# Modulation steps of three chunks on GpSimd's queue, and products that move from GpSimd to VectorE and ScalarE

## The chip, the core and the metric

The kernel runs on one core of a Trainium2 chip. TensorE (PE in the profile) multiplies matrices, VectorE (DVE) and ScalarE (ACT) work on rows of 128 partitions, GpSimd (POOL) does both arithmetic and the issuing of transfers, and SyncE (SP) only issues transfers. The metric is the device time of one execution in microseconds (us), lower is better; the time of a kernel is the median of its runs.

## The reference

Two residual networks run one after the other on 256 tokens of width 1024, all in float32. The first has two layers of differential attention beside a Hyena convolution. The second has an even layer (forgetting attention and gated linear attention, then a dense SwiGLU) and an odd layer (an s5 state-space mixer, then a mixture of eight experts). Every sublayer of the second network is modulated by a conditioning vector `c`:

```python
def adaln(c, w, b):
    m = jax.nn.silu(c.astype(jnp.float32)) @ w + b      # w: 1024 x 3072
    shift, scale, gate = jnp.split(m, 3, axis=-1)
    return shift[:, None, :], scale[:, None, :], gate[:, None, :]

def second_block(x, c, ...):
    # four modulations: e_mod_mix, e_mod_ffn, o_mod_mix, o_mod_ffn
    sh, sc, g = adaln(c, e_mod_mix_w[j], e_mod_mix_b[j])
    h = rmsnorm(x, e_norm_mix[j]) * (1.0 + sc) + sh
    y = even_mixer(h, ...)
    x = x + (g * y).astype(x.dtype)
    # then the same with the dense swiglu, the s5 mixer and the experts
```

The modulations depend on `c` alone, so they may be computed at any time before their use. The s5 mixer's parameters (powers of a complex decay, two matrices B and C per state, tables of cosines and sines) depend on weights alone, and may also be computed early.

## The kernel before

The text of the program is turned into one instruction list per engine by a scheduler that simulates the engines; an engine then works through its list in order. Weights arrive on SyncE's queue as [128 x 1024] chunks (`wchunk`). Each is split into a high part `whi` on ACT (L207) and a low part `wlo` on DVE (L210), and each product is three matmuls (L220 to L222, and L322 to L324 where the weight stands still).

By the trace, the first network runs until about 570 us, the even mixer from 640 to 765 us, the dense SwiGLU (the dense FFN below) from about 765 to 1010 us, the s5 mixer from 1060 to 1200 us, and the experts fill the rest.

**Background tasks.** Work that isn't due yet is written as a Python generator. `tick()` is called after each piece of a projection and lets each task take `rate` steps; `finish()` runs a task to its end. The four modulations are such a task (`modulations`, `adaln`) within the first network, at a rate of 0.65 steps for each tick, and `self.finish(self.adalns)` stands ahead of `w_out` of the first network's second layer. One modulation is 24 chunks of [128 x 1024]. A step takes two chunks (`ADA_STEP`). A chunk is fetched by SyncE's queue into `rawm` (L942, three buffers), and multiplied in eight pairs of instructions, 16 on PE in the profile's count (L947). After each four chunks ACT copies the result (L952), PE transposes it in four pieces (L955), and DVE adds up (L956). At the end of a modulation PE transposes the gate (L963), and a DMA writes it out as a row, from which GpSimd's queue later broadcasts `mgt` to all partitions (L200). A modulation has 13 steps; with the eight that are skipped at the start there are 60.

**The s5 parameters** are a task beside the even mixer and the dense FFN. For each of four quarters q it computes B (L1461 transposes, L1463 masks), C (four complex products by `cmul`, L1330 to L1338, on DVE, then masks L1477 and L1483 on POOL) and the tables T. A table is built by six complex products that double its length, all on POOL, and its one buffer is stored to memory as `sT` (L1522) by SyncE's queue before the next quarter's may be begun (POOL sets its first column at L1514, ACT fills its third part at L1520).

**The mixers.** In the gated linear attention POOL multiplies `gz` by `gq` and `gk` (L1104, L1105, L1132) and `gg` by `gn` (L1225). In the s5 mixer it does four additions per quarter beside two scans of DVE (L1559, L1562, L1575, L1576).

Of the kernel before, what the change touches and what calls it, by code (L numbers as in the profile page):

```python
# [118 lines left out]
class Net:  # L119
    def __init__(self, ctx, tc, a, out):  # L120
        self.ctx, self.tc, self.nc, self.a, self.out = ctx, tc, tc.nc, a, out
        self.uid, self.ring, self.extra, self.left, self.hold, self.held = 0, {}, 0, 0, None, 0
        self.tasks = []
        self.dq = (tc.nc.gpsimd, tc.nc.sync, tc.nc.scalar)[DQ]
# [801 lines left out]
    def adaln(self, key, pool, raw_alloc):  # L926
# [8 lines left out]
        bc = self.load(self.sm, a[key + "_c"], [P, 4, 8], "adb", bufs=1, eng=self.dq)  # L935
        ad = self.t(self.sm, [P, 24], "adv", bufs=1)
        silu = self.silu_cols(pool)
        for m0 in range(0, 24, 4):
            acc = self.psB()
            for m in range(m0, m0 + 4):  # L940
                raw = raw_alloc()
                nc.sync.dma_start(raw, w[m])  # L942
                cs = slice((m - m0) * P, (m - m0 + 1) * P)
                for r in range(2):
                    for j in range(4):
                        k = 2 * j + r
                        nc.tensor.matmul(acc[32 * j:32 * j + 32, cs], silu[:, k:k + 1].broadcast_to([P, 32]),  # L947
                                         raw[:, k * P:(k + 1) * P], start=r == 0 and m == m0, stop=r == 1, skip_group_check=True)
# [7 lines left out]
            V.tensor_reduce(ad[:, m0:m0 + 4], pt.rearrange("p (m j r) -> p m j r", m=4, j=4)[:, :, :, 0], AX.X, ALU.add)  # L956
            yield
        V.tensor_tensor(cols[:, 1], ad[:, 0:8], bc[:, 0], ALU.add)
# [7 lines left out]
        self.dq.dma_start(row.rearrange("(m n) -> m n", n=P), r)  # L966
# [13 lines left out]
    def modulations(self):  # L980
        raw = lambda: self.t(self.b1, [P, D], "rawm", bufs=AR_BUFS)
        for _ in range(ADA_SKIP):
            yield
        for k in ("e_mod_mix", "e_mod_ffn", "o_mod_mix", "o_mod_ffn"):
            yield from self.adaln(k, self.b1, raw)
            if k == "e_mod_ffn":
                for _ in range(ADA_SKIP1):
                    yield

    def adaln_task(self, key, pool, rate):  # L990
        return self.task(self.adaln(key, pool, self.raw), rate)
# [74 lines left out]
    def gla(self, b2, qT, kT, v, la, gg, yT):  # L1066
# [28 lines left out]
        for lv in range(6):  # L1095
# [8 lines left out]
            nc.gpsimd.tensor_tensor(zv[:, :, h:], zv[:, :, h:], qf.rearrange("p (n t) -> p n t", t=B)[:, :, h:], ALU.mult)  # L1104
            nc.gpsimd.tensor_tensor(zv[:, :, :h], zv[:, :, :h], kf.rearrange("p (n t) -> p n t", t=B)[:, :, :h], ALU.mult)  # L1105
# [6 lines left out]
        for lv in (6, 7):  # L1112
# [17 lines left out]
            for c in range(4):  # L1130
                second = c % 2 if lv == 6 else c // 2
                nc.gpsimd.tensor_tensor(zv[:, :, c, :], zv[:, :, c, :], (q4 if second else k4)[:, :, c, :], ALU.mult)  # L1132
# [30 lines left out]
    def even_mixer(self, b2):  # L1163
# [56 lines left out]
        def emit_gg(tt, c, p):  # L1220
# [4 lines left out]
            nc.gpsimd.tensor_tensor(v4, v4, gn[:, None, :].broadcast_to([P, 4, P]), ALU.mult)  # L1225
# [206 lines left out]
    def s5_params(self, sp):  # L1432
# [8 lines left out]
        for q in range(4):  # L1441
# [28 lines left out]
            for t in range(4):  # L1470
# [11 lines left out]
            for g in range(2):  # L1482
                nc.gpsimd.tensor_tensor(cm[:, 0, :, g, :], craw[:, 0], m2[:, None, g, :].broadcast_to([P, 8, 16]), ALU.mult)  # L1483
# [579 lines left out]
```

## Time and profile before

| | |
|---|---|
| Median of 3 runs | 1993.03 us (1983.26 to 1996.6) |
| The profiled execution | 1992.76 us, of which the span is 1991.0 us |
| Granted TensorE clock, mean of the span | 0.95 |
| PE, DVE, ACT, POOL busy | 94%, 78%, 60%, 10% |

The profiled execution is within the runs. Busy shares are means over stages with different limits, so the rows below are cut by stage. A matmul's listed length overlaps the next one's; how far PE moved is read from the starts. In a row of the timeline the bracket at the end is the time for which the engine was idle before, and what ended that.

### The profile page before, as it was taken

How to read it: one execution, taken by the hardware profiler on the slowest of the kernel's cores; microseconds unless marked ns; L12 is line 12 of the kernel's file. 1: busy time of each engine (PE TensorE's matmuls, PEld its weight loads, DVE VectorE, ACT ScalarE, POOL GpSimd, SP SyncE). 2: the span in 40 equal slices, each digit the busy share in tenths (PEclk: the TensorE clock that was granted, in tenths of full speed). 3: DMA queues.
4: the chain of work that ended last, by engine and by line, in shares of the span. 5: the costliest groups of instructions: out<-in, count | busy, mean ns of one | idle time of the engine just before them, and what ended most of it. 6: DMA issues, size and time to landing. Idle time of an engine off the chain costs nothing.

```text
span 1991.0 us, 31217 instructions
## 1 busy us (share of the span) xinstructions
PE 1869.4 (94%) x11450; PEld 1580.4 (79%) x11450; DVE 1555.7 (78%) x2484; ACT 1190.1 (60%) x1628; POOL 196.9 (10%) x319
## 2 busy tenths in 40 slices
PE   7899989999976998889988989999999999999997
PEld 6787767887754977779978978888888888888875
DVE  6687577686432756788878678999999999999897
ACT  6564445554322843434445358787788877877775
POOL 0000000000010011872212210010001000100000
PEclk9999999999977987999999789999999999999999
DMA  8635656755687631557666568999999999999991
GB/s 259 193 121 171 209 177 210 253 161 191 221 280 237 174 102 51 173 210 234 216 238 251 216 238 282 374 323 377 352 369 316 379 353 378 324 382 357 356 346 57
DMA packets 254826, 503.37 MB, mean 253 GB/s; under 512 B 20082, under 2 KB 97396, under 8 KB 252616
## 3 DMA queue, kind: packets, MB, share of 16 engines
q1 hardware_dynamic: 253848, 498.47, 72.5%
q0 software_dynamic: 816, 2.82, 0.4%
q8 instruction: 92, 1.51, 0.3%
q14 instruction: 70, 0.57, 0.1%
HBM read 485.47 MB, written 15.75 MB: 252 GB/s over the span
## 4 chain that ended last, share of the span: by engine, by line
PE 77%; DVE 8%; DMA 6%; issue 3%; POOL 3%; ACT 3%; SPq 0%; ACTq 0%; DVEq 0%; POOLq 0%
PE A L220 12%; PE A L222 12%; PE A L221 12%; PE B L220 6%; PE B L221 6%; PE B L222 6%; PE A L322 3%; PE A L323 3%; PE A L324 3%; PE B L947 3%; DVE wlo L210 2%; DMA k<-in_flt_deltas_dram 1%; DMA rawm<-in_o_mod_ffn_w_dram 1%; PE B L1743 1%; PE B L439 1%
## 5 line engine op out<-in xcount | busy, mean ns | idle before, releaser
L210 DVE TENSOR_TENSOR wlo<-raw,whi 128x1024 fp32r<-128x1024 f32 x777 | 935.0, 1227 | 190.1 <-ACT whi L207 178.7
L207 ACT ACTIVATE whi<-raw 128x1024 fp32r<-128x1024 f32 x777 | 813.5, 1057 | 369.9 <-PE A L222 141.6
L221 PE MATMUL A<-wlo,hTh 128*128 128x512 f32 (+1 forms) x752 | 288.6, 384 | 1.6 <-DVE wlo L210 1.3
L220 PE MATMUL A<-whi,hTh 128*128 128x512 f32 (+1 forms) x752 | 285.4, 387 | 4.2 <-ACT hTh L207 4.2
L222 PE MATMUL A<-whi,hTl 128*128 128x512 f32 (+1 forms) x752 | 286.9, 383 | 0.9 <-DVE hTl L210 0.9
L322 PE MATMUL A<-hTh,whi 128*128 128x256 f32 x864 | 248.4, 288 | 7.7 <-ACT whi L207 4.3
L324 PE MATMUL A<-hTh,wlo 128*128 128x256 f32 x864 | 246.6, 285 | 1.4 <-DVE wlo L210 1.4
L323 PE MATMUL A<-hTl,whi 128*128 128x256 f32 x864 | 246.8, 286 | 1.0 <-DVE hTl L210 1.0
L322 PEld LDWEIGHTS A<-hTh,whi 128*128 128x128 f32 x864 | 167.1, 193 | 12.0 <-ACT whi L207 4.5
L323 PEld LDWEIGHTS A<-hTl,whi 128*128 128x128 f32 x864 | 167.3, 194 | 3.6 <-issue 1.4
L324 PEld LDWEIGHTS A<-hTh,wlo 128*128 128x128 f32 x864 | 167.2, 193 | 3.7 <-DVE wlo L210 1.8
L220 PEld LDWEIGHTS A<-whi,hTh 128*128 128x128 f32 x752 | 141.7, 189 | 35.4 <-ACT hTh L207 4.9
L221 PEld LDWEIGHTS A<-wlo,hTh 128*128 128x128 f32 x752 | 141.8, 189 | 33.3 <-DVE wlo L210 4.9
L222 PEld LDWEIGHTS A<-whi,hTl 128*128 128x128 f32 x752 | 142.0, 189 | 31.0 <-DVE hTl L210 2.0
L221 PE MATMUL A<-wlo,xg 128*128 128x512 f32 (+1 forms) x384 | 143.5, 374 | 0.0
L222 PE MATMUL A<-whi,xg 128*128 128x512 f32 (+1 forms) x384 | 143.0, 372 | 0.0
L220 PE MATMUL A<-whi,xg 128*128 128x512 f32 (+1 forms) x384 | 141.7, 376 | 0.0
L221 PE MATMUL B<-wlo,mhh 128*128 128x512 f32 x352 | 138.7, 394 | 0.0
L222 PE MATMUL B<-whi,mhl 128*128 128x512 f32 x352 | 137.6, 391 | 0.0
L220 PE MATMUL B<-whi,mhh 128*128 128x512 f32 x352 | 120.9, 394 | 0.2 <-ACT mhh L207 0.2
L947 PE MATMUL B<-rawm,silu 128*32 128x128 f32 x1536 | 70.8, 312 | 22.0 <-DMA rawm<-in_o_mod_ffn_w_dram 14.3
L947 PEld LDWEIGHTS B<-rawm,silu 128*32 128x32 f32 x1536 | 45.0, 122 | 47.8 <-DMA rawm<-in_o_mod_ffn_w_dram 20.6
(575 smaller groups left out, 2974.1 us busy)
## 6 DMA issues: line engine op xcount, KB each, us to landing
raw<-in_o_exp_up_dram SPq DMA_DIRECT2D x176, 512.0 KB, 5.8
raw<-in_o_exp_down_dram SPq DMA_DIRECT2D x176, 512.0 KB, 6.1
raw<-in_o_exp_gate_dram SPq DMA_DIRECT2D x174, 512.0 KB, 5.7
raw<-in_w_in_dram SPq DMA_DIRECT2D x96, 512.0 KB, 5.1
rawm<-in_e_mod_mix_w_dram SPq DMA_DIRECT2D x24, 512.0 KB, 3.7
rawm<-in_e_mod_ffn_w_dram SPq DMA_DIRECT2D x24, 512.0 KB, 6.6
rawm<-in_o_mod_mix_w_dram SPq DMA_DIRECT2D x24, 512.0 KB, 4.9
raw<-in_e_w_in_dram SPq DMA_DIRECT2D x24, 512.0 KB, 4.2
```

Source lines behind the costliest of these rows:

```text
L207: nc.scalar.activation(hi, src, AF.Copy)
L210: (nc.gpsimd if lo_eng == "pool" else nc.vector).tensor_tensor(lo, src, hi.bitcast(F32), ALU.subtract)
L220: nc.tensor.matmul(out, ah, bh, start=first, stop=False)
L221: nc.tensor.matmul(out, ah, bl, start=False, stop=False)
L222: nc.tensor.matmul(out, al, bh, start=False, stop=last)
L322: nc.tensor.matmul(o, wh[:, ms], xh[:, k, :], start=k == 0 and m == 0, stop=False, **kw)
L323: nc.tensor.matmul(o, wh[:, ms], xl[:, k, :], start=False, stop=False, **kw)
L324: nc.tensor.matmul(o, wl[:, ms], xh[:, k, :], start=False, stop=k == 7, **kw)
L439: nc.tensor.matmul(o, x[:, ks], dg, start=True, stop=True)
L947: nc.tensor.matmul(acc[32 * j:32 * j + 32, cs], silu[:, k:k + 1].broadcast_to([P, 32]), raw[:, k * P:(k + 1) * P], start=r == 0 and m == m ...
L1743: nc.tensor.transpose(ptr[:, i * P:(i + 1) * P], sg[:, i * P:(i + 1) * P], self.ident)
```

## The change

1. **Modulations.** A step is now three chunks, and nothing is yielded inside it. The next step's three chunks are issued on GpSimd's queue (`self.mq`) right after this step's matmuls. The matmuls and ACT's copy of [128 x 384] are written under high priority. In place of four transposes per four chunks, four small DMAs of GpSimd's queue put one row of each of the four partial sums into `parts` [96 x 128], and one transpose and one reduction per modulation finish it. A modulation is 10 steps; with the eight skipped there are 48. The rate is 0.80. The three buffers of `rawm` stay.
2. **Gated linear attention.** The products with `gq`, `gk` and `gn` go to DVE.
3. **s5 parameters.** The masks of C (72 operations on [128 x 128]) go to ACT as copies with a scale per partition. The complex products of the tables T go to DVE, 144 operations.
4. **s5 mixer.** The four additions per quarter go to DVE.

Lines in the changed file are one to eleven higher (L947 is L959, the new DMAs are L965, the one transpose is L970). The core of the diff:

```diff
-    def adaln(self, key, pool, raw_alloc):
+    def adaln(self, key, pool, raw_alloc, bufs):
...
+        parts = self.t(self.sm, [96, P], "adp", bufs=1)
...
-        for m0 in range(0, 24, 4):
+        def fetch(m0):
+            raws = [raw_alloc() for _ in range(bufs)]
+            for i in range(bufs):
+                self.mq.dma_start(raws[i], w[m0 + i])
+            return raws
+
+        raws = fetch(0)
+        yield
+        for m0 in range(0, 24, bufs):
             acc = self.psB()
-            for m in range(m0, m0 + 4):
-                raw = raw_alloc()
-                nc.sync.dma_start(raw, w[m])
-                cs = slice((m - m0) * P, (m - m0 + 1) * P)
-                for r in range(2):
-                    for j in range(4):
...
-                if m % ADA_STEP == ADA_STEP - 1 and m < m0 + 3:
-                    yield
-            s = self.t(pool, [P, 512], "ads", bufs=1)
-            nc.scalar.activation(s, acc, AF.Copy)
-            pt = self.psB()
-            for i in range(4):
-                nc.tensor.transpose(pt[:, i * P:(i + 1) * P], s[:, i * P:(i + 1) * P], self.ident)
-            V.tensor_reduce(ad[:, m0:m0 + 4], ...)
+            with self.first():
+                for i in reversed(range(bufs)):
+                    cs = slice(i * P, (i + 1) * P)
+                    for r in range(2):
+                        for j in range(4):
...
+                s = self.t(pool, [P, bufs * P], "ads", bufs=1)
+                nc.scalar.activation(s, acc[:, :bufs * P], AF.Copy)
+            for j in range(4):
+                self.mq.dma_start(parts[24 * j + m0:24 * j + m0 + bufs], s[32 * j:32 * j + 1].rearrange("o (m p) -> o m p", m=bufs))
+            if m0 + bufs < 24:
+                raws = fetch(m0 + bufs)
             yield
+        pt = self.psB()
+        nc.tensor.transpose(pt[:, 0:96], parts, self.ident[0:96, 0:96])
+        V.tensor_reduce(ad, pt[:, 0:96].rearrange("p (j m) -> p m j", j=4), AX.X, ALU.add)
...
-            nc.gpsimd.tensor_tensor(zv[:, :, h:], zv[:, :, h:], qf..., ALU.mult)
+            nc.vector.tensor_tensor(zv[:, :, h:], zv[:, :, h:], qf..., ALU.mult)
...
-                        nc.gpsimd.tensor_tensor(C[:, :, ri, t, g, :], v, m2[:, None, g, :].broadcast_to([P, 8, 16]), ALU.mult)
+                        nc.scalar.activation(C[:, :, ri, t, g, :], v, AF.Copy, scale=m2[:, g, 0:1])
...
-                          T[:, 0, :, n:2 * n], T[:, 1, :, n:2 * n], f"s5rt", eng=nc.gpsimd)
+                          T[:, 0, :, n:2 * n], T[:, 1, :, n:2 * n], f"s5rt")
...
-            nc.gpsimd.tensor_tensor(t[0], t[0], t[1], ALU.add)
+            V.tensor_tensor(t[0], t[0], t[1], ALU.add)
...
-ADALN_RATE = 65
+ADALN_RATE = 80
```

**How the order moves.** First PE's list where the first network ends and the even mixer begins. `rawm` is a fetched chunk, `silu` the conditioning vector, `ads` the copied partial sums, `dg` and `x` the normalised input of the next projection, `adb` the gate. Before:

```order
L947 MATMUL B_6110<-rawm_6111,silu_1532 32x128 x8
L947 MATMUL B_6110<-rawm_6121,silu_1532 32x128 x8
L947 MATMUL B_6110<-rawm_6131,silu_1532 32x128 x8
L947 MATMUL B_6110<-rawm_6141,silu_1532 32x128 x8
L955 MATMUL B_6153<-ident_78,ads_6151 128x128 x4
L963 MATMUL B_6163<-ident_78,adb_5862 8x128
L439 MATMUL B_6361<-dg_6359,x_75 128x128 x4
```

The changed kernel at the last modulation step, within `w_out`'s matmuls (L221 to L223 are its three matmuls), and then at the end of `w_out`:

```order
L221 MATMUL A_6272<-whi_6306,hTh_6082 128x512
L959 MATMUL B_6149<-rawm_6145,silu_1264 32x128 x8
L959 MATMUL B_6149<-rawm_6144,silu_1264 32x128 x8
L959 MATMUL B_6149<-rawm_6143,silu_1264 32x128 x8
L222 MATMUL A_6272<-wlo_6307,hTh_6082 128x512
```

```order
L223 MATMUL A_6273<-whi_6306,hTl_6083 128x512
L970 MATMUL B_6180<-ident_78,adp_5451 128x96
L977 MATMUL B_6187<-ident_78,adb_5448 8x128
L440 MATMUL B_6385<-dg_6383,x_75 128x128 x4
L440 MATMUL B_6397<-dg_6383,x_75 128x128 x4
```

Before, the list holds modulation steps alone between `w_out` and the next layer's input; now the last step's three chunks stand 23 matmuls ahead of `w_out`'s end, and two transposes are left behind it.

Second, GpSimd's own list in the first network, changed kernel. `adp` is the tile `parts`. Before, the list there has no such rows:

```order
L965 DMA adp_1263<-ads_2120 3x1x128 x4
L945 DMA rawm_2238<-in_e_mod_mix_w_dram 128x1024
L945 DMA rawm_2239<-in_e_mod_mix_w_dram 128x1024
L945 DMA rawm_2240<-in_e_mod_mix_w_dram 128x1024
L965 DMA adp_1263<-ads_2232 3x1x128 x4
```

The scheduler put each fetch (here 2238 to 2240) ahead of the small DMAs of the step whose buffers it takes over (`ads_2232`): the three chunks wait for that step's matmuls, not for ACT's copy.

Third, SyncE's list in the dense FFN, at the store of the first quarter's table. Before:

```order
L264 DMA raw_8287<-in_e_ffn_down_dram 128x1024
L194 DMA s5b_8889<-in_s5b_dram 128x2x128
L1522 DMA sT_6685<-s5T_8787 128x1536
L264 DMA raw_8293<-in_e_ffn_down_dram 128x1024
L264 DMA raw_8382<-in_e_ffn_gate_dram 128x4x256
```

and in the changed kernel:

```order
L265 DMA raw_8607<-in_e_ffn_down_dram 128x1024
L265 DMA raw_8682<-in_e_ffn_gate_dram 128x4x256
L265 DMA raw_8688<-in_e_ffn_gate_dram 128x4x256
L1533 DMA sT_6709<-s5T_8811 128x1536
L265 DMA raw_8750<-in_e_ffn_up_dram 128x4x256
```

The store now stands behind more of the dense FFN's weights. DVE's list of the changed kernel shows where the table's products (`s5rt`) went, between those of C (`s5cm`) and the low parts of weights:

```order
L1341 TENSOR_TENSOR s5rt_1882_9431<-s5T_9428,s5cos_6969 128x8
L1342 TENSOR_TENSOR s5rt_1883_9432<-s5T_9428,s5sin_6968 128x8
L1347 SCALAR_TENSOR_TENSOR s5ci_8569<-s5cm_1709_8572,s5cm_1710_8573 128x128
L1343 TENSOR_TENSOR s5rt_1884_9433<-s5T_9428,s5sin_6968 128x8
L1344 TENSOR_TENSOR s5rt_1885_9434<-s5T_9428,s5cos_6969 128x8
L211 TENSOR_TENSOR wlo_8610<-raw_8607,whi_8609 128x1024
```

They were on POOL before, and DVE had none of them.

## Rows read from the trace of the kernel before

**Rows 1.** Part 1 of the page: busy time, share of span, instructions

```profile
PE 1869.4 (94%) x11450; PEld 1580.4 (79%) x11450; DVE 1555.7 (78%) x2484; ACT 1190.1 (60%) x1628; POOL 196.9 (10%) x319
```

**Rows 2.** Windows by stage: stretch, length, busy by engine, granted clock, DMA share, GB/s

```profile
570.00:636.00 66.00, 38.79 (x550) 23.91 (x549) 8.37 (x43) 9.35 (x19) 6.07 (x8) 0.64 0.78 264
...
765.00:1010.00 245.00, 223.50 (x1515) 206.83 (x1512) 196.49 (x408) 105.28 (x138) 117.31 (x233) 0.94 0.59 192
```

**Rows 3.** PE's timeline, end of first block: start, length, line, operation, [idle before]

```profile
569.62 0.40 PE L222 MATMUL A<-whi,hTl 128*128 128x512 f32 x1
...
632.64 0.93 PE L947 MATMUL B<-rawm,silu 128*32 128x128 f32 x16 [2.61 <-DMA rawm<-in_o_mod_ffn_w_dram]
...
643.04 0.50 PE L222 MATMUL A<-whi,hTl 128*128 128x512 f32 x1 [0.87 <-DVE hTl L210]
```

**Rows 4.** Windows of L947 alone: PE busy, weight-load busy, clock, DMA share, GB/s

```profile
0.00:536.00 536.00, 35.22 (x860) 23.12 (x864) 0.98 0.60 195
...
570.00:636.00 66.00, 29.55 (x512) 17.80 (x512) 0.64 0.78 264
```

**Rows 5.** PE's timeline where layer 0 turns to layer 1

```profile
288.17 0.39 PE L222 MATMUL A<-whi,hTl 128*128 128x512 f32 x1
...
306.52 0.50 PE L222 MATMUL A<-whi,hTl 128*128 128x512 f32 x1
```

**Rows 6.** PE's timeline, modulation work within the projection flow

```profile
547.35 0.60 PE L955 MATMUL B<-ident,ads 128*128 128x128 f32 x4
547.88 1.52 PE L947 MATMUL B<-rawm,silu 128*32 128x128 f32 x48
549.33 0.50 PE L220 MATMUL A<-whi,hTh 128*128 128x512 f32 x1
...
549.66 0.40 PE L221 MATMUL A<-wlo,hTh 128*128 128x512 f32 x1
549.90 0.40 PE L222 MATMUL A<-whi,hTl 128*128 128x512 f32 x1
```

**Rows 7.** DMA issues on GpSimd's queue: destination, source, count, KB each, us to landing

```profile
mgt<-rowe_mod_ffn POOLq DMA_DIRECT2D x1, 512.0 KB, 3.8
...
xg<-in_final_norm_dram POOLq DMA_DIRECT2D x1, 512.0 KB, 7.6
```

**Rows 8.** POOL's groups: count, busy us, mean ns, idle before

```profile
L200 POOL DMA_DIRECT2D mgt<-rowo_mod_mix x1 | 0.6, 597 | 28.3 <-DVE sm L332 28.3
```

**Rows 9.** Waits in 765:870: engine, line, awaited, us in total, times, longest

```profile
ACT s5T L1520 <- DMA sT<-s5T: 17.8, 3, 8.7
...
PE B L1461 <- DVE s5st L1463: 8.6, 2, 6.6
```

**Rows 10.** DVE's groups in 765:1010, by form

```profile
L210 DVE TENSOR_TENSOR wlo<-raw,whi 128x1024 fp32r<-128x1024 f32 x65 | 83.1, 1281 | 32.4 <-ACT whi L207 32.0
...
L1332 DVE TENSOR_TENSOR s5cm<-s5pw,s5c 128x128 f32<-128x128 f32 x16 | 6.7, 416 | 0.1
...
L1332 DVE TENSOR_TENSOR s5cm<-s5pw,s5W 128x128 f32<-128x128 f32 x12 | 3.8, 317 | 0.0
```

**Rows 11.** DVE's groups in 640:765, by form

```profile
L1102 DVE TENSOR_TENSOR gz<-gb 128x256 f32<-128x256 f32 x6 | 2.5, 418 | 0.0
...
L1332 DVE TENSOR_TENSOR s5cs<-s5pw,s5v 128x32 f32<-128x32 f32 x3 | 0.5, 174 | 0.0
```

**Rows 12.** POOL's groups, whole span

```profile
L1104 POOL TENSOR_TENSOR gz<-gz,gq 128x256 f32<-128x256 f32 x6 | 5.4, 903 | 133.0 <-ACT gq L1213 109.9 <-ACT gz L1103 23.1
```

**Rows 13.** Timeline, POOL and DVE side by side in the dense FFN

```profile
794.35 0.21 POOL L1332 TENSOR_TENSOR s5rt<-s5T,s5sin 128x16 f32<-128x16 f32 x1
794.35 1.28 DVE L210 TENSOR_TENSOR wlo<-raw,whi 128x1024 fp32r<-128x1024 f32 x1
794.52 1.19 POOL L1333 TENSOR_TENSOR s5rt<-s5T,s5cos 128x16 f32<-128x16 f32 x1
```

**Rows 14.** Windows by engine inside the s5 mixer

```profile
1095.00:1120.00 25.00, 25.00 (x126) 24.77 (x125) 21.44 (x32) 6.38 (x18) 8.41 (x8) 0.55 0.31 119
```

More of the change, by code (lines that the diff above doesn't have):

```diff
@@ L934, in adaln @@
         row = self.rows[key] = self.t(self.dram, [D], "row" + key)
-        bc = self.load(self.sm, a[key + "_c"], [P, 4, 8], "adb", bufs=1, eng=self.dq)
+        bc = self.load(self.sm, a[key + "_c"], [P, 4, 8], "adb", bufs=1, eng=self.mq)
         ad = self.t(self.sm, [P, 24], "adv", bufs=1)
+        parts = self.t(self.sm, [96, P], "adp", bufs=1)
         silu = self.silu_cols(pool)
-        for m0 in range(0, 24, 4):
-            acc = self.psB()
-            for m in range(m0, m0 + 4):
-                raw = raw_alloc()
-                nc.sync.dma_start(raw, w[m])
-                cs = slice((m - m0) * P, (m - m0 + 1) * P)
-                for r in range(2):
-                    for j in range(4):
-                        k = 2 * j + r
-                        nc.tensor.matmul(acc[32 * j:32 * j + 32, cs], silu[:, k:k + 1].broadcast_to([P, 32]),
-                                         raw[:, k * P:(k + 1) * P], start=r == 0 and m == m0, stop=r == 1, skip_group_check=True)
-                if m % ADA_STEP == ADA_STEP - 1 and m < m0 + 3:
-                    yield
-            s = self.t(pool, [P, 512], "ads", bufs=1)
-            nc.scalar.activation(s, acc, AF.Copy)
-            pt = self.psB()
-            for i in range(4):
-                nc.tensor.transpose(pt[:, i * P:(i + 1) * P], s[:, i * P:(i + 1) * P], self.ident)
-            V.tensor_reduce(ad[:, m0:m0 + 4], pt.rearrange("p (m j r) -> p m j r", m=4, j=4)[:, :, :, 0], AX.X, ALU.add)
@@ new lines, in fetch @@
+        def fetch(m0):
[6 more added lines that the diff above has]
+        for m0 in range(0, 24, bufs):
+            acc = self.psB()
+            with self.first():
[3 more added lines that the diff above has]
+                        for j in range(4):
+                            k = 2 * j + r
+                            nc.tensor.matmul(acc[32 * j:32 * j + 32, cs], silu[:, k:k + 1].broadcast_to([P, 32]),
+                                             raws[i][:, k * P:(k + 1) * P], start=r == 0 and i == bufs - 1, stop=r == 1,
+                                             skip_group_check=True)
+                s = self.t(pool, [P, bufs * P], "ads", bufs=1)
[4 more added lines that the diff above has]
+                raws = fetch(m0 + bufs)
@@ L965, in adaln @@
         nc.scalar.copy(r, pt[0:8, 0:P])
-        self.dq.dma_start(row.rearrange("(m n) -> m n", n=P), r)
+        self.mq.dma_start(row.rearrange("(m n) -> m n", n=P), r)
         yield
@@ L984, in modulations @@
         for k in ("e_mod_mix", "e_mod_ffn", "o_mod_mix", "o_mod_ffn"):
[L985 to L988, printed above, removed]
+            yield from self.adaln(k, self.b1, raw, AR_BUFS)
     def adaln_task(self, key, pool, rate):
-        return self.task(self.adaln(key, pool, self.raw), rate)
+        return self.task(self.adaln(key, pool, self.raw, 2), rate)
     def gate_row(self, key):
@@ L1574, in states @@
                 nc.gpsimd.memset(X[i][:, :, 0:1], 0.0)
-            nc.gpsimd.tensor_tensor(X[0][:, :, 1:], v8(t[0]), v8(t[1]), ALU.subtract)
-            nc.gpsimd.tensor_tensor(X[1][:, :, 1:], v8(t[2]), v8(t[3]), ALU.add)
+            V.tensor_tensor(X[0][:, :, 1:], v8(t[0]), v8(t[1]), ALU.subtract)
+            V.tensor_tensor(X[1][:, :, 1:], v8(t[2]), v8(t[3]), ALU.add)
             held[q] = X, Uq
@@ L2059 @@
 HOLDC = 0
-ADA_STEP = 2
 ADA_SKIP = 8
-ADA_SKIP1 = 0
```

13 lines of the change are left out of this document (7 added, 6 removed).

## The prediction, made before the changed kernel was run

> **What bounds the kernel now.** I first read the page's list of busy times: PE is busy for 94% of the span [rows 1], so a stage gets shorter where PE has less to do, or waits less, and other engines count where PE waits for them. Then I cut the span into windows by stage. Two stand out [rows 2]. From 570 to 636 us PE is busy for only 38.8 of 66 us, at a granted clock of 0.64, and no other engine is busy for more than 10. From 765 to 1010 us, the dense FFN, PE idles for 245 − 223.5 = 21.5 us, and DVE is busy for 196.5 (80%). PE's timeline tells what the first is: `w_out`'s last matmul starts at 569.62, and the next product of a layer's flow that runs on without a break at 643.04 [rows 3]. Between them lie modulation chunks, each waiting for its own transfer (2.61 us in the row shown). The window of that line alone counts 512 records there, at 16 a chunk 32 chunks, and 860 (some 54 chunks) before 536 us [rows 4]; the last ten lie between. So a third of the modulations runs as a tail that nothing covers.
>
> **The tail goes.** The new rate and the shorter steps let all 48 steps end inside the projections: in PE's order the last three chunks stand 23 matmuls ahead of `w_out`'s end. What is left at that place is a turn from one layer to the next. The turn from layer 0 to layer 1, with the same norm, transposes and first weights, takes from 288.17 to 306.52, 18.4 us [rows 5]. So 73.4 us become 18.4: **−55**. Bounds: −47, if the turn takes 8 us more, since the two new transposes wait for small DMAs there; −61, if it takes 12, as the turn of layer 0 also holds 1 us of modulation work and other stops.
>
> **The 32 chunks of the tail move into the flow.** Within the flow three chunks take from 547.88 to 549.33, 1.45 us, so 0.48 a chunk [rows 6]: 32 × 0.48 = 15.5 us. In exchange the four transposes per four chunks go; a group takes 547.35 to 547.88, 0.53 us, and some 15 of the 24 stand in the flow (the tail has the others, and went with it): −8. Sum **+7.5**. Bounds: +15.5 if the transposes had filled idle time; +3 if some moved chunks fill the turn between the layers.
>
> **Late fetches.** The three buffers stay, so the next three chunks can be fetched only when this step's matmuls are done, and all are needed at once. Before, SyncE ran one or two chunks ahead. A fetch on GpSimd's queue is nowhere in this trace for `rawm`; the nearest rows are 512 KB that GpSimd's queue broadcasts: 3.8 to 7.6 us to landing [rows 7], 0.6 us for an issue [rows 8]. Three issues and one landing are 5.6 to 9.4 us; I take 7.5, the middle, since SyncE's weights share the transfer engines in this stage (195 GB/s at a share of 0.60 [rows 4]). Against that stand the distances between steps in PE's order, each matmul of the flow taken at 0.24 us (549.66 to 549.90 [rows 6]) and the others by their columns. Of 31 distances the nine shortest are 3.8, 5.8, 6.5, 7.6, 7.7, 7.8, 8.6, 8.7 and 9.2 us, then come thirteen from 9.4 to 11.1. PE's shortage is the sum of what is missing: at 7.5 it is 3.7 + 1.7 + 1.0 = **+6.5**; at 5.6 it is 2; at 9.4 it is 19. The distances leave out PE's own waits, so the true ones are somewhat longer and the shortage rather smaller. While PE waits there, the flow's matmuls stand behind it, so I count the shortage in full. The four small DMAs per step don't delay the fetch: GpSimd's list has the fetch ahead of them.
>
> **Dense FFN.** The tables' 144 products come to DVE: four quarters of six complex products, each with operations on 128 x 8 to 128 x 256. Rows for DVE at the sizes: 0.174 us at 32 columns, 0.317 at 128, 0.418 at 256 [rows 10, 11]. With 0.17 for 8 and 16 columns and 0.25 for 64, a quarter has 6 × (3 × 0.17 + 0.25 + 0.32 + 0.42) = 9.0 us: +36 on DVE. It gets relief where POOL's work held it: the same complex product takes 416 ns beside POOL's masks and 317 without [rows 10]; 96 such operations × 0.1 give −10, and some low parts of weights −3. DVE rises from 196.5 to about 219 of 245 us, 90%. ACT takes 72 masks on 128 x 128, estimated at 0.4 us each as DVE's operations of that size [rows 10], 28 us onto 105 of 245 [rows 2]: covered by its idle time; without that cover, the high parts of weights would come later and the price would be up to those 28. On the other side the waits behind the table's store shrink. It blocks ACT for 17.8 us, and PE waits 8.6 for DVE's masks of B [rows 9]. The store now stands nine weights later in SyncE's list, so the same wait may come back on DVE; I let PE's idle 21.5 us lose 8, and add 4 for DVE's greater load: **−4**, between −13 (the store's waits gone altogether) and +15 (below).
>
> **Mixers.** A product of `gz` takes 0.90 us on POOL and a subtraction of the same size 0.42 on DVE [rows 11, 12]; twelve of them at 0.5 less are 6 us on a chain that is partly covered: **−2**, between −6 and +2 (DVE's own queue). In the s5 mixer PE runs at a clock of 0.55 from 1095 to 1120 us and is busy throughout, DVE for 21.4 of 25 [rows 14]; sixteen additions of twice the size above, an estimated 0.84 us each on DVE (twice 0.42) for 1.8 on POOL (twice 0.90): 0, between −8 (a better clock) and +6 (DVE's queue full).
>
> **Sum**: −55 + 7.5 + 6.5 − 4 − 2 = −47 against the profiled execution's 1992.8, which is the median of the runs to 0.3 us: **1946 us**.
>
> **Rivals.**
>
> *DVE becomes the bound of the dense FFN.* Its low parts of weights wait 32.4 us for ACT [rows 10]; 196.5 + 32.4 + 23 = 252, which is 7 more than the stage lasts, and the table's wait of 17.8 moves from ACT to DVE and holds up the low parts. Then the stage costs +7 to +25 in place of −4: 1957 to 1975 us. For it: DVE's list mixes the table's products with those of C and the low parts. Against it: much of those 32.4 us can be filled. Chance 0.09.
>
> *DVE holds up the fetches' issue.* A POOL product took 1.19 us beside a low part of 1.28, and 0.21 before it [rows 13], so an operation of POOL can stand until DVE's is done. If each of three issues lost 0.98 so, the fetch would take 10.4 us and the shortage would be 32: +26 over my sum, 1972 us. Against it: an issue took 0.597 us in a stage in which DVE was working [rows 8], and an issue has no large operand. The Trainium skill (SBUF — State Buffer, in the section on its two separate sides, the box on DVE blocking DMA) warns of this: transfers from GpSimd's queue have their descriptors written by GpSimd's cores, which stand still while VectorE holds the shared port in a two-port mode, and it advises SyncE's or ScalarE's queue. By that rule this change would lose most in the first network; the issue of 0.597 us does not agree with it, and no row here shows a fetch beside it. Chance 0.10.
>
> *The other side: three fetches at once are too slow.* One mechanism: 1.5 MB asked for in one go, beside SyncE's stream, on the same transfer engines. From 570 to 636 us these moved 264 GB/s at a share of 0.78 [rows 2]. If the fetch got under half of that, 115 GB/s, 1.5 MB would take 13 us. Then 24 distances are too short, the shortage is 91, and the sum +38: 2030 us. It decides from 11.4 us on, where the shortage (54) eats up all the rest, and over 1% from 12.3. For it: the nearest landing rows are single transfers. Against: their worst is 7.6. Chance 0.07.
>
> *Better than forecast*: PE keeps its clock where the additions on POOL had held it up, and the flow gains by SyncE's free queue: under 1920, chance 0.05. That the change doesn't do what it says is excluded by the order, where each step's matmuls stand together and no step is left behind `w_out`.
>
> **Numbers.** My own sum has 0.69: most of it within 1920 to 1975. The range that holds 8 in 10 takes in the rivals up to the held-up issue and part of the slow fetch: **1920 to 1985**. A measurement of this kernel tells 1% (20 us) from no change: faster means below 1973, slower above 2013. Faster: my sum's 0.65, DVE's 0.08, the better case's 0.05 and 0.04 of the held-up issue, **0.82**; slower 0.06 (the slow fetch), the same **0.12**.
>
> **What would show it.** Right: no stretch with modulation steps alone after `w_out`, and about 18 us between its last matmul and the even mixer's flow; waits of PE for `rawm` in the first network of 2 to 19 us in total; landings of `rawm` at 4 to 8 us; DVE some 220 us busy in the dense FFN. Wrong: waits for `rawm` above 50 us, issues on POOL of over 1 us, waits of DVE for the table's store, or a dense FFN of over 250 us.

## The result, and the profile after

The changed kernel takes 1910.42 us (median of 5 runs, 1902.7 to 1913.79) against 1992.71 before (5 runs): a ratio of 0.9592, 95% interval 0.9558 to 0.9626, or 82 us less. The forecast was 1946 with a range of 1920 to 1985: the sign was right, the size too small, and the time lies below the range. The profiled execution, 1902.7 us with a span of 1900.2, is the fastest of the five, so its sum below comes to 91 us rather than 82.

Part 1 of the page, to be held against [rows 1]:

```profile
PE 1818.4 (96%) x11358; PEld 1551.7 (82%) x11358; DVE 1554.9 (82%) x2646; ACT 1213.4 (64%) x1708; POOL 164.6 (9%) x297
```

PE is busy for 51 us less and idle for some 40 less. DVE has 162 instructions more and is busy for as long as before (1555.7 in [rows 1]): that is the first surprise.

PE's timeline at the end of the first network, which answers to [rows 3]:

```profile
555.66 1.52 PE L959 MATMUL B<-rawm,silu 128*32 128x128 f32 x48 [1.13 <-DMA rawm<-in_o_mod_ffn_w_dram]
...
562.34 0.40 PE L223 MATMUL A<-whi,hTl 128*128 128x512 f32 x1
563.71 0.27 PE L970 MATMUL B<-ident,adp 96*128 96x96 f32 x1 [0.96 <-PE A L223]
564.84 0.27 PE L977 MATMUL B<-ident,adb 128*8 128x128 f32 x1 [0.87 <-DVE sm L333]
566.56 3.00 PE L440 MATMUL B<-dg,x 128*128 128x128 f32 x16 [1.45 <-DVE sm L342]
572.13 0.79 PE L221 MATMUL A<-whi,hTh 128*128 128x512 f32 x1 [2.57 <-ACT whi L208]
```

The tail is gone: the last step stands inside `w_out`, and ten microseconds lie between `w_out`'s last matmul and the next projection's first. To the matmul that the prediction had named (643.04 before) it is 11.8 us in place of 73.4; three of these 62 us are lost again by the even mixer's flow (645.94 before). `w_out` ends at 562.34, 7 us earlier than in [rows 3], though 32 more chunks lie before it. That is the second surprise.

Windows over the work that filled the dense FFN's 765 to 1010 us before, and over the two modulation lines up to `w_out`'s end: first all engines as in [rows 2], then L959 alone as in [rows 4], then the new transposes (L970) alone:

```profile
701.40:922.40 221.00, 215.28 (x1514) 200.89 (x1513) 194.05 (x552) 126.71 (x211) 5.34 (x17) 0.97 0.66 215
...
0.00:563.00 563.00, 50.30 (x1536) 41.52 (x1536) 0.98 0.71 233
...
0.00:563.00 563.00, 0.74 (x3) 0.42 (x3) 0.98 0.71 233
```

The last two for the kernel before, L947 and the transposes L955 alone, up to its `w_out`'s end:

```profile
0.00:570.00 570.00, 41.20 (x1024) 27.23 (x1024) 0.98 0.61 200
...
0.00:569.80 569.80, 8.98 (x60) 7.31 (x60) 0.98 0.62 200
```

In the dense FFN PE idles for 5.7 us in place of 21.5, and DVE is busy for 194.1 in place of 196.5, though 144 products have come to it.

**Where the 91 us of the profile are.** Both kernels run the same 7824 matmuls with split weights (those that read `whi` or `wlo`). I took the start of the k-th of them in either trace, at seven points, and the difference from point to point. Points of the kernel before: `w_out`'s end (569.62), the even mixer's flow under way (645.94), within the dense FFN before its stops (829.56) and behind them (941.61), within the s5 mixer (1067.11 and 1116.79), and the last (1974.03); "end" is what follows. One row per kernel, in us against the kernel before; the kernels are those of the experiments below:

```
             network 1  its end  mixer  FFN    to s5   s5    rest   end
changed         -7.3    -58.4    -4.5  -15.9   0.1  -10.2    1.7    3.8
mod_only        -4.4    -57.2    -5.8    7.0   0.0    0.0    0.0    3.8
prod_only       -0.9      4.8     1.1  -14.3  -1.7  -10.2    1.0   -0.2
rate_alone      23.5    -59.1    -4.3    5.5   4.8    0.0    0.4   -0.2
pool_fetch      21.4    -58.9    -5.8    6.7   0.1    0.0   -0.5    2.0
rate65         -11.3     -1.1     2.8  -14.3   1.7  -11.1    2.1    3.5
sync_fetch       6.7    -57.9     2.7  -14.2  -1.5  -10.2    1.1   -0.2
sync_raw        -0.9    -58.1     1.8  -14.3   1.7   -9.8    3.6   -0.2
sync_small       5.4    -58.4     8.1  -14.3   1.8  -11.2    2.1    2.4
tab_back        -9.2    -57.6     4.1   -5.2  -1.5  -10.2    1.7    3.5
tab_bufs2       -8.6    -58.6     3.0   -4.9  -1.7  -10.2    1.5    3.5
tab_copy        -7.6    -57.2     4.3   -8.8  -1.6  -10.0    1.4    3.5
mask_back       -5.7    -58.8     1.5  -12.0  -0.1  -10.2    1.6    3.5
add_back        -8.1    -58.6     2.9  -15.8   0.0    0.0   -0.4    3.5
after_bufs2     -8.6    -58.4     2.8  -12.7   0.2   -9.8    1.7    3.5
after_copy      -7.0    -57.5    -4.5  -15.5  -0.1  -10.2    1.5    3.8
before_copy      0.2      1.9    -2.7   -4.7  -1.8    0.0   -2.5   -0.2
```

Against the sum of the forecast (network 1: +14, its end: -55, dense FFN: -4, mixers: -2 and 0), the end of the network held; the network itself missed by 21, the dense FFN by 10 to 12 and the s5 mixer by 7 to 10. Two columns need care.

*s5.* With the additions on DVE a block of 32 matmuls (L1565) comes behind this column's last point instead of ahead of it. Up to a matmul behind that block in either kernel (1129.7 us before) the gain is 6.8 us, and by 1229 us it is 8.6.

*mixer.* This column runs to within the dense FFN and holds a loss and a gain. The loss lies where the gated linear attention's products went to DVE. From 645.94 to 730.18 us the same matmuls take 84.2 us in the five kernels that leave these products on GpSimd (before, mod_only, rate_alone, pool_fetch, before_copy), 86.7 in the changed kernel and after_copy, and 91.0 to 97.7 in the other eleven. PE's idle time at its end, from 719 to 730 us, is 3.0 us in all thirteen and 0.2 in the five. Windows there, of the kernel before, the changed one and mask_back, and below them how the second product of `gg` (L1236) stands in the changed kernel's list ahead of the reciprocal that PE waits for:

```profile
717.00:735.00 18.00, 15.59 (x88) 11.44 (x86) 12.67 (x32) 8.57 (x20) 4.02 (x4) 1.00 0.32 98
```

```profile
650.00:672.00 22.00, 16.64 (x96) 11.93 (x94) 14.72 (x40) 9.20 (x23) 0.00 (x0) 1.00 0.32 93
...
656.12 0.69 DVE L1236 TENSOR_TENSOR gg<-gg,gn 128x512 f32<-128x512 f32 x1
...
656.92 0.16 DVE L1062 RECIPROCAL sm<-sm 128x1 f32<-128x1 f32 x1
...
657.16 0.30 PE L1066 MATMUL B<-ident,fx_s 128*128 128x128 f32 x1 [1.76 <-DVE sm L1062]
```

```profile
650.00:674.00 24.00, 20.45 (x93) 14.76 (x91) 13.68 (x37) 9.12 (x20) 0.00 (x0) 0.79 0.23 69
```

The clock that PE was granted stayed at its upper level in the changed kernel's profile (1.00) and fell for a part of the stretch in mask_back's (a mean of 0.79), as in ten others. So this part of the change costs 2.5 us in the profile shown and 7 to 10 in most; no run moved these products alone, so that they are the cause is argued from the thirteen and the five. Behind 730 us 3 to 7 us come back in every version. The 86.7 us against 91.0 to 93.9 (sync_small aside) are 4 to 7 of the 8 us by which the profiled execution is faster than the median.

### The profile page after: what moved, and what is told of

The parts are those of the page before. It is cut to its first block, busy times and chain, and to the rows that moved or that the text cites. A ratio compares the mean times of both kernels' runs of the same rounds, so it can differ in the third digit from the quotient of the medians.

```text
span 1900.2 us, 31269 instructions
## 1 busy us (share of the span) xinstructions
PE 1818.4 (96%) x11358; PEld 1551.7 (82%) x11358; DVE 1554.9 (82%) x2646; ACT 1213.4 (64%) x1708; POOL 164.6 (9%) x297
## 4 chain that ended last, share of the span: by engine, by line
PE 78%; issue 10%; DVE 6%; DMA 4%; ACT 2%; POOL 0%; POOLq 0%; ACTq 0%; DVEq 0%
PE A L222 12%; PE A L221 12%; PE A L223 12%; PE B L221 6%; PE B L222 6%; PE B L223 6%; PE A L323 4%; PE A L325 4%; PE A L324 4%; PE B L959 2%; DMA rawm<-in_e_mod_mix_w_dram 2%; DVE wlo L211 1%; PE B L1754 1%; PE B L1101 1%; PE B L440 1%
## 5 line engine op out<-in xcount | busy, mean ns | idle before, releaser
L221 PE MATMUL A<-whi,hTh 128*128 128x512 f32 (+1 forms) x752 | 286.7, 389 | 7.5 <-ACT hTh L208 4.9
L223 PE MATMUL A<-whi,hTl 128*128 128x512 f32 (+1 forms) x752 | 287.5, 384 | 0.9 <-DVE hTl L211 0.9
L221 PEld LDWEIGHTS A<-whi,hTh 128*128 128x128 f32 x752 | 142.9, 190 | 38.8 <-ACT hTh L208 6.1
L223 PEld LDWEIGHTS A<-whi,hTl 128*128 128x128 f32 x752 | 142.6, 190 | 31.2 <-DVE hTl L211 2.1
L223 PE MATMUL A<-whi,xg 128*128 128x512 f32 (+1 forms) x384 | 142.7, 372 | 0.0
L221 PE MATMUL A<-whi,xg 128*128 128x512 f32 (+1 forms) x384 | 141.2, 375 | 0.0
L223 PE MATMUL B<-whi,mhl 128*128 128x512 f32 x352 | 137.5, 391 | 0.0
L221 PE MATMUL B<-whi,mhh 128*128 128x512 f32 x352 | 120.6, 393 | 0.2 <-ACT mhh L208 0.2
L222 PEld LDWEIGHTS A<-wlo,xg 128*128 128x128 f32 x384 | 72.3, 188 | 13.4 <-DVE wlo L211 0.8
L223 PEld LDWEIGHTS A<-whi,xg 128*128 128x128 f32 x384 | 72.3, 188 | 12.5
```

Of the source, the lines that this page charges most:

```text
L221: nc.tensor.matmul(out, ah, bh, start=first, stop=False)
L222: nc.tensor.matmul(out, ah, bl, start=False, stop=False)
L223: nc.tensor.matmul(out, al, bh, start=False, stop=last)
```

## Experiments

**The two halves.** mod_only is the changed kernel with all products back on GpSimd; prod_only is the kernel before with the products moved:

```diff
-nc.vector.tensor_tensor(zv[:, :, h:], zv[:, :, h:], qf..., ALU.mult)      # and gk, gn
+nc.gpsimd.tensor_tensor(zv[:, :, h:], zv[:, :, h:], qf..., ALU.mult)
-nc.scalar.activation(C[:, :, ri, t, g, :], v, AF.Copy, scale=m2[:, g, 0:1])
+nc.gpsimd.tensor_tensor(C[:, :, ri, t, g, :], v, m2[:, None, g, :].broadcast_to([P, 8, 16]), ALU.mult)
-T[:, 1, :, n:2 * n], f"s5rt")
+T[:, 1, :, n:2 * n], f"s5rt", eng=nc.gpsimd)
-V.tensor_tensor(t[0], t[0], t[1], ALU.add)                                # and the other three
+nc.gpsimd.tensor_tensor(t[0], t[0], t[1], ALU.add)
```

> The modulations' part alone: steps of three chunks by GpSimd's queue, rate 0.80, one transpose; all products stay on GpSimd as before. Theory A (the two parts add up, and each works in its own stage): -66 us up to the even mixer, as the matched matmuls of the profiles show (-7 within the first network, -58 at its end), and nothing later, so 1925 us. Rival B (the gain after 765 us, too, comes from the modulations, as SyncE's queue or the clock is in another state by then): 1905 to 1915 us. My prediction's own sum for this part: -41, 1951 us.

> The products' part alone: gated linear attention, masks of C, tables T and the s5 additions leave GpSimd; the modulations as before, tail included. Theory A: -25 us (from 765 us on), so 1968 us. Rival B: the -6 of the prediction or less, 1985 to 1993 us.

Measured: mod_only 1934.66 us (ratio 0.9699, 0.9661 to 0.9738), prod_only 1970.24 us (0.9892, 0.9849 to 0.9934). That is 3.0% and 1.1%, together 4.1%, the whole of it. By the times Theory A holds: the parts add up. The prediction had 41 and 6 us where 60 and 21 were measured. But mod_only came out 10 us above the 1925 us expected, and the table says where: in the dense FFN it is 7.0 us longer than the kernel before, as rate_alone and pool_fetch are by 5.5 and 6.7. PE waits there for DVE's masks of B, 8.6 us before [rows 9] and more in mod_only:

```profile
PE B L1472 <- DVE s5st L1474: 15.1, 5, 6.4
```

In the changed kernel and in prod_only PE has no such wait in that stretch. So the products' part is worth 14 us there by itself and 23 beside the new modulations; the two parts are not independent in that stretch.

**The rate alone**, on the kernel before:

```diff
-ADALN_RATE = 65
+ADALN_RATE = 110
```

> The kernel before with one number changed: the modulations' rate goes from 0.65 to 1.10 steps a tick, so that the order holds no tail (the last two chunks stand inside w_out); steps stay two chunks, SyncE fetches, four transposes per four chunks. Theory A (the tail's removal is the gain; broken steps cost 0.59 us a chunk and 0.4 a chunk for its transposes): 32 chunks come into the flow at 0.8 to 1.0 us, +26 to +32, against -58 at the end of the network: -26 to -32, so 1961 to 1967 us. Rival C (unbroken steps and GpSimd's queue add nothing): as the modulations' part alone, about 1925 us. Rival D (SyncE's queue, held by more fetches, brings weights late): 1980 us or more.

Measured: 1958.35 us (0.9813, 0.9769 to 0.9856), by Theory A. More than half of the modulation part's gain is one number. The tail is worth 57 to 59 us whoever removes it, and 23.5 of them are paid back in the network. Windows of the chunks (L947) and of the transposes (L955) alone, up to `w_out`'s end:

```profile
0.00:594.00 594.00, 56.68 (x1536) 39.76 (x1536) 0.98 0.68 219
...
0.00:594.00 594.00, 14.48 (x96) 11.48 (x96) 0.98 0.68 219
```

With unbroken steps and one transpose the same two rows were 50.30 and 0.74 us: 20 us of busy PE are what the new form of the step saves in the flow, of the 28 by which the first networks of rate_alone and mod_only differ.

**The chunks by GpSimd's queue**, beside the rate alone:

```diff
-                nc.sync.dma_start(raw, w[m])
+                nc.gpsimd.dma_start(raw, w[m])
-ADALN_RATE = 65
+ADALN_RATE = 110
```

> The kernel before with the rate at 1.10 and, beside that, the modulations' chunks fetched by GpSimd's queue; steps of two chunks and four transposes stay. Theory D (SyncE's queue, which stood for over 90 us of the first network before fetches, is freed for the weights): the first network is 10 to 14 us shorter than with the rate alone, 1944 to 1949 us. Rival K (the queue doesn't matter; what separates the rate alone from the whole modulation part, some 24 us, is the broken steps and the transposes): 1955 to 1962 us.

Measured: 1957.05 us (0.9851, 0.9819 to 0.9883), and 2 us less than rate_alone within the network: Rival K. With broken steps the queue alone gives next to nothing; of its profile's 35 us less, nearly all is the rate's.

**The queue in the changed kernel**, in four corners: all on GpSimd's queue (the changed kernel), all on SyncE's (sync_fetch), the chunks alone there (sync_raw), or the small DMAs, biases and rows alone (sync_small):

```diff
-        self.mq = tc.nc.gpsimd                                  # sync_fetch, sync_small
+        self.mq = tc.nc.sync
-                self.mq.dma_start(raws[i], w[m0 + i])           # sync_raw; sync_small: nc.gpsimd
+                nc.sync.dma_start(raws[i], w[m0 + i])
```

> The changed kernel with the fetches and the small DMAs of the modulations on SyncE's queue in place of GpSimd's. Theory A (the queue doesn't matter as long as PE seldom waits): 1905 to 1918 us, as the changed kernel. Rival D (in the kernel before, SyncE stood for 77 us of the first network before fetches whose buffers were still in use, and the weights behind them came late, which is where the unforeseen -7 came from): the first network gets 10 to 30 us longer, 1920 to 1940 us. Rival E (GpSimd's queue is the slower one): 1900 us or less.

> The changed kernel with the chunks fetched by SyncE's queue, but the small DMAs, the biases and the rows left on GpSimd's. With all of them on SyncE's queue the first network was 14 us longer in the profile. Theory D (the fetches stand before buffers in use and hold up the weights and filter loads behind them): the 14 us stay, the first network ends 5 to 9 us later than in the kernel before; 1916 to 1924 us. Rival N (the small DMAs, which wait for ACT's copy, do the holding up): the first network is as in the changed kernel, 1906 to 1914 us.

> The changed kernel with the chunks on GpSimd's queue, and the small DMAs, biases and rows on SyncE's. Theory D (chunks that wait for a buffer hold up the weights behind them): the first network as in the changed kernel, ending 5 to 9 us before that of the kernel before; 1906 to 1914 us. Rival N (the small DMAs, which wait for ACT's copy, hold them up): it ends some 6 us later, 1914 to 1920 us.

Measured: sync_fetch 1918.85 us (0.961, 0.9564 to 0.9655), sync_raw 1914.99 (0.9602, 0.9548 to 0.9657), sync_small 1923.72 (0.9651, 0.9621 to 0.968). By their times only the last stands nearly clear of the changed kernel; it lies above both expectations, the other two between theirs. By the matched matmuls the network is 14, 6 and 13 us longer than in the changed kernel, while all ten profiles with everything on GpSimd's queue and steps of three lie between -4.4 and -11.3. So both theories hold a part: chunks that wait for a buffer cost 6, and small DMAs, which wait for ACT, 13; together they cost 14, so the two do not add up. Each of the three figures is from one profile. SyncE's waits (its queue, line, what it waited for: us, times, longest) up to `w_out`'s end, in the kernel before, the changed one and sync_small:

```profile
SPq L264 <- DVE wlo L210: 196.1, 76, 8.6
SPq L942 <- PE B L947: 92.4, 34, 8.9
```

```profile
SPq L265 <- DVE wlo L211: 321.2, 87, 24.1
```

```profile
SPq L265 <- DVE wlo L211: 159.8, 73, 6.3
SPq L965 <- ACT ads L963: 63.1, 21, 6.8
```

A SyncE that waits for a weight buffer to come free (`wlo`) is ahead of the engines that use the weights; this slack is 321 us where no modulation work stands in its list, and 196 or 160 where it does. The wait before a fetch was in plain sight before. The prediction had it only as one of two grounds of a better case.

**The rate of 0.65 in the changed kernel**, which leaves seven steps as a tail:

> The changed kernel at the old rate, 0.65: by the order seven steps, 21 chunks, are left as a tail behind the last covered work. Theory A (the tail is paid per step, since each waits for its own fetch with nothing beside it): before, 32 chunks took some 55 to 60 us more than a bare turn, 1.8 us a chunk; here a step of three is a fetch of about 7.5 us plus 1.5 us, 3.0 us a chunk, so 7 x 9 = 63 us, less 21 x 0.5 = 10 in the flow: +53, 1955 to 1970 us. Rival M (transfers are shared out better by GpSimd's queue, as in the tail before, 1.8 us a chunk): 38 less 10, +28, 1930 to 1942 us.

Measured: 1963.49 us (0.9863, 0.981 to 0.9917), +53 over the changed kernel: Theory A. PE's timeline there:

```profile
566.99 2.79 PE L959 MATMUL B<-rawm,silu 128*32 128x128 f32 x48 [6.81 <-DMA rawm<-in_o_mod_ffn_w_dram]
577.24 2.79 PE L959 MATMUL B<-rawm,silu 128*32 128x128 f32 x48 [7.47 <-DMA rawm<-in_o_mod_ffn_w_dram]
585.67 2.79 PE L959 MATMUL B<-rawm,silu 128*32 128x128 f32 x48 [5.64 <-DMA rawm<-in_o_mod_ffn_w_dram]
```

A step costs 8.4 to 10.3 us when nothing covers its fetch, 2.7 us a chunk by the table (57 us over 21 chunks). It is dearer than before's tail (58 us over 32 chunks, 1.8 a chunk), where a step took two of the three buffers. The new step is cheap only where the rate keeps it inside the flow.

**Which products, and where.** Each of three parts goes back to GpSimd alone, with the edits shown above:

> The changed kernel, but the tables T stay on GpSimd. Theory F (a ring of waits: before, DVE's next product of C stood 4.8 us before GpSimd's masks, GpSimd's list stood before the store of a table, and PE stood 8.6 us before DVE; it takes both the masks and the tables on GpSimd): with the masks gone the ring stays open, and at 829 to 870 us (before's time) nearly all of the 16 us stay gained; 1906 to 1915 us. Rival G (the gain there is that GpSimd's products no longer hold up DVE's): 144 products return to GpSimd, half of the 16 us comes back, 1917 to 1922 us.

> The changed kernel, but the masks of C stay on GpSimd. Theory F: the masks alone have no store ahead of them, and the 16 us stay gained; 1906 to 1915 us, with DVE's products of C at some 0.42 us again in place of 0.29. Rival G: 96 products of C at 0.13 us more and the wait for masks, half of the 16 us comes back, 1917 to 1922 us. Rival H (the masks on ACT hold up the high parts of weights): 1900 us or less.

> The changed kernel, but the s5 mixer's sixteen additions stay on GpSimd. Theory I (the 10 us between 1057 and 1117 us of before come from these additions alone: they held DVE's scans, 2.02 us in place of 1.22, and PE's clock fell while PE waited): 10 us come back, there alone; 1918 to 1922 us. Rival J (another part of the products, or the earlier work in another order, made that gain): within 4 us of the changed kernel.

Measured: tab_back 1921.05 us (0.9663, 0.9634 to 0.9691), mask_back 1913.1 (0.9603, 0.9568 to 0.9638), add_back 1915.84 (0.9624, 0.9595 to 0.9654). By their times neither mask_back nor add_back stands apart from the changed kernel, and 1915.84 lies between the two expectations for add_back. The profile decides for Theory I: with the additions back on GpSimd nothing of the s5 mixer's gain is left, nor with all products there (mod_only); with the additions on DVE it is there under the old modulations, too (prod_only). Windows over the same matmuls of the s5 mixer, before, changed and add_back, and the scan of DVE (L1575) in the changed kernel and in add_back:

```profile
1067.00:1129.70 62.70, 57.09 (x402) 56.52 (x401) 53.65 (x86) 24.08 (x55) 23.11 (x20) 0.78 0.47 173
```

```profile
980.90:1036.80 55.90, 53.06 (x400) 52.92 (x399) 51.46 (x98) 23.80 (x55) 0.45 (x4) 0.85 0.54 192
...
L1575 DVE TENSOR_TENSOR_SCAN s5t<-sqT,s5t 128x512 f32<-128x512 f32 x4 | 4.9, 1219 | 0.0
```

```profile
987.40:1051.00 63.60, 57.70 (x405) 56.97 (x403) 53.77 (x86) 24.29 (x55) 23.11 (x20) 0.79 0.47 172
...
L1575 DVE TENSOR_TENSOR_SCAN s5t<-sqT,s5t 128x512 f32<-128x512 f32 x4 | 8.1, 2022 | 1.7 <-POOL s5t L1570 1.7
```

PE stands idle for 2.8 us in place of 5.6 and is busy for 4.0 us less: the mean of its granted clock is 0.85 in place of 0.78, and the same matmuls spend less of the stretch at the lower of the two clock levels. Most of that is one block of 32 matmuls (L1554 before), which took 7.29 us right behind the longest stop, where each of the three such blocks now takes 3.68.

In the dense FFN PE is idle between the table's two points for 10.8 us before and for none in the changed kernel; the other 5 us are busy time, at a mean granted clock of 0.98 in place of 0.94. With the tables on GpSimd 7.3 us of idle time are back, with the masks on GpSimd 1.9. Of the masks' other 2 us in the table nothing can be said, since after_bufs2, with everything moved and no idle time there, shows -12.7, too. Theory F (a ring of waits which either part alone would open) fell: with the masks on ACT and the tables on GpSimd most of the gain was gone.

**Why the tables.** Two buffers for a table; the copy into its third part moved from ACT to GpSimd, each with and without the tables' products:

```diff
-T = self.t(sp, [P, 3, 8, 64], "s5T", bufs=1)          # tab_bufs2 (tables on GpSimd), after_bufs2
+T = self.t(sp, [P, 3, 8, 64], "s5T", bufs=2)
-nc.scalar.copy(T[:, 2], bc(mg4, 64))                  # tab_copy (tables on GpSimd), after_copy, before_copy
+nc.gpsimd.tensor_copy(T[:, 2], bc(mg4, 64))
```

> The changed kernel with the tables T on GpSimd, and two buffers for a table in place of one, so that the next quarter's table need not wait for the store of the last. With one buffer this version lost 11 of the 16 us that the changed kernel gains in the first part of the dense FFN. Theory L (it is the wait for the store that costs: ACT's copy into the table stands before it, and with it the high parts of weights): 10 us or more come back, 1906 to 1913 us. Theory G (GpSimd's 144 products hold up DVE's operations): nothing comes back, 1917 to 1924 us.

> The changed kernel with two buffers for a table. Theory L: with the tables on DVE PE no longer waits there in the profile, so a second buffer has nothing left to give: 1906 to 1914 us. A gain beyond that (1900 us or less) would say that the store's wait still costs something on DVE or ACT.

> The changed kernel with the tables' products on GpSimd and, beside that, the copy into the third part of the table moved from ACT to GpSimd. Theory P (ACT stood before this copy, and the high parts of weights behind it): the dense FFN gets its 11 us back, 1908 to 1914 us. Theory G (GpSimd's products hold up DVE's operations): nothing comes back, 1917 to 1925 us.

> The kernel before with that copy alone moved from ACT to GpSimd, all else as it was. Theory P: 8 to 12 us less in the dense FFN, 1977 to 1982 us. Theory G: no change, 1986 to 1994 us.

> The changed kernel with that copy moved from ACT to GpSimd; its products are on DVE. Both theories: within 4 us of the changed kernel, 1906 to 1914 us, since ACT's waits for the table cost PE little there. Below 1903 us would say that ACT's copy still cost something.

Measured: tab_bufs2 1922.82 us (0.9672, 0.9617 to 0.9727), after_bufs2 1911.84 (0.9601, 0.9552 to 0.965), tab_copy 1917.05 (0.9632, 0.9602 to 0.9662), before_copy 1987.61 (0.9979, 0.9964 to 0.9994), after_copy 1907.44 (0.9586, 0.9551 to 0.962). Theory L fell: a second buffer gives nothing. Waits from 765 to 820 us, of tab_back (one buffer) and of tab_bufs2, and below them DVE's low parts of weights in the latter's same stretch and in the changed kernel's whole dense FFN (695 to 925 us), there with a product of C:

```profile
ACT s5T L1531 <- DMA sT<-s5T: 18.4, 2, 12.2
DVE wlo L211 <- ACT whi L208: 10.8, 2, 10.6
```

```profile
ACT s5T L1531 <- POOL s5rt L1341: 9.4, 1, 9.4
...
L211 DVE TENSOR_TENSOR wlo<-raw,whi 128x1024 fp32r<-128x1024 f32 x15 | 24.1, 1613 | 5.1 <-ACT whi L208 5.0
```

```profile
L211 DVE TENSOR_TENSOR wlo<-raw,whi 128x1024 fp32r<-128x1024 f32 x66 | 80.6, 1222 | 15.3 <-ACT whi L208 14.7
...
L1343 DVE TENSOR_TENSOR s5cm<-s5pw,s5c 128x128 f32<-128x128 f32 x16 | 4.6, 285 | 0.0
```

ACT changes what it waits for, from the store to GpSimd's products, and stands either way. Moving ACT's copy out of that wait brings 4 us of the dense FFN back (-8.8 for -5.2), and 5 us in the kernel before (-4.7). So Theory P has about 4 to 5 of the tables' 10 us. What is left (-8.8 against -15.9) points to Theory G: beside the tables on GpSimd a low part takes longer. But the 1.61 us are the worst case. Over the whole column a low part takes 1.22 us in the changed kernel, 1.26 in tab_back, 1.30 in tab_copy and 1.41 in tab_bufs2; in tab_copy that is some 2 us on 31 low parts, and PE's stops there are 4.6 us. So the rest of the tables' gain stays open. after_copy is the fastest version that was run, but it isn't apart from the changed kernel (0.9586 and 0.9592).

## Why the prediction was wrong

The sign was right, the tail's removal came as foreseen, and none of the three rivals on the slow side came. The step that failed is the sizing of the other terms: four were mis-sized, all towards too little gain, one had the wrong sign, and one was left out.

- **The tail**, -55: held. -58 in the profile, -57 to -59 in fourteen kernels without a tail; and with a tail again (rate65) it was all back.
- **The chunks in the flow**, +7.5: +1. By the windows of the two lines, 50.30 + 0.74 us for 96 chunks against 41.20 + 8.98 for 64 before. I had priced new chunks at the best of the old ones (0.48) and had not seen that the old 64, in broken steps, cost 41.20 / 64 = 0.64 each and fell to 50.30 / 96 = 0.52.
- **Late fetches**, +6.5: +1.6. PE's waits before `rawm` in the first network, 3.7 us in the changed kernel and 2.1 before:

```profile
PE B L959 <- DMA rawm<-in_e_mod_mix_w_dram: 2.6, 3, 1.3
...
PE B L959 <- DMA rawm<-in_o_mod_ffn_w_dram: 1.1, 1, 1.1
```

```profile
PE B L947 <- DMA rawm<-in_o_mod_mix_w_dram: 2.1, 1, 2.1
```

  The fetch of three chunks, from its first issue to its last landing, took 8.1 us in the median (6.6 to 10.8), near the 7.5 assumed (issues of 0.54, median landings of 5.6 to 6.3 by modulation). So the distances were longer than counted, as the text had allowed.
- **SyncE's freed queue**: not in the sum. For the chunks it is worth 6 us beside the new steps (sync_raw) and 2 beside the old ones (pool_fetch). The small DMAs, which cost more on that queue, are new and explain nothing against the kernel before. With the two terms above these 6 us make 17 of the 21 us that the network missed; the other 4 have no cause here.
- **Dense FFN**, -4: -16, and -12.7 to -15.9 in all kernels with tables and masks moved. Of PE's 21.5 us of idle time I had let 8 go; 15.8 went, and its busy time fell, too. DVE's added work was right (144 products), its relief was not. The 317 ns that I took as undisturbed were themselves disturbed, since the undisturbed size is 285 to 290, and 219 us of DVE in the sum became 194. Nor did I count ACT's wait for the table, which ended in the same move, or the stops that the new modulations add where the products stay.
- **Even mixer**, -2: a loss of 2.5 us in the profile and of 7 to 10 in most others, where the bound was +2. I had set the operations' lengths against each other (0.90 and 0.42 us); what the trace shows is that they now stand in DVE's list ahead of operations for which PE waits (3.0 us idle in place of 0.2). What came back behind them hides this in the table.
- **s5 mixer**, 0: -7 to -9, at the bound of -8. I had weighed additions against additions (0.84 against 1.8 us), where the scan beside them was the price: 2.02 to 1.22 us.
- **Rivals.** DVE did not become the bound. GpSimd's issue wasn't held up: 96 fetches took 527 to 561 ns each, 65 of them beside a TENSOR_TENSOR of DVE. The rule of the Trainium skill that I had weighed (SBUF — State Buffer, the box on DVE blocking DMA) speaks of DVE's two-port modes; no trace here shows that DVE ran in one beside a fetch, so these runs do not test it. The same page's section "Who interferes with whom" says that a DVE operation with two inputs in SBUF and a GpSimd operation that reads SBUF exclude each other; the scans (2.02 and 1.22 us) and the products of C (0.42 and 0.285) agree, and that is the rule which should have set the relief. The slow fetch did not come: the longest landing was 9.7 us.
- **The range.** Its lower end lay 26 us below the sum, although the six bounds on that side (6, 4.5, 4.5, 9, 4 and 8 us) made 36 together, and the better case, with both its grounds, got 0.05.

## What to carry to other kernels

Background work that is left as a tail costs its latency, not its work: count the ticks before choosing another form of the step, since the rate alone gave more than half of this part. Where operations leave an engine beside which another's took longer, size the relief by the same operation's shortest time anywhere in the trace, and look at the longest operation beside them, not only at those that move. Where operations come to an engine, look for what stands behind them in its list and who waits for that: the products of the gated linear attention seem to cost more than they gave, though the changed kernel with these alone left on GpSimd was not run. A transfer that must wait for a buffer or for another engine belongs on a queue with nothing urgent behind it; read that from the queue's own waits.

## What the runs showed that I had not expected

The end of the program got longer. From the last output's issue to the end of the span it takes 5.9 us in the kernel before (8 DMAs on GpSimd's queue) and in sync_fetch (8), 5.95 in sync_raw (144, all small), 8.1 and 8.6 in pool_fetch and sync_small (104, of which 96 are chunks), and 9.6 in the changed kernel (240). So 3.7 us of the gain are lost behind the last output in the changed kernel, and 2 to 4 in each version with the chunks on that queue; why, the traces don't tell.
